# Dividing a ring of thirteen buffers among three kinds of tile, and issuing the loads of a unit earlier, in a chunked RWKV-7 scan

## The chip, the cores and the metric

The kernel runs on one core of a Trainium2 chip. The metric is the device time of one execution in microseconds (us). Three executions of the kernel before gave 4045.82, 4052.56 and 4052.54 us; their median is 4052.54. One more execution was taken with the hardware profiler; it took 4050.69 us, and every row below is from that one.

A core has five engines that follow their own instruction streams: PE (TensorE, matmuls; its weight loads are listed apart as PEld), DVE (VectorE), ACT (ScalarE), POOL (GpSimd) and SP (SyncE, which here issues nearly all DMAs). Each stream runs strictly in its own order. Streams meet at semaphores.

## The reference

A trunk of two layers works on 512 latent tokens and 256 context tokens of 1024 channels. Every layer is a half-SwiGLU, a token mixer, and another half-SwiGLU. Layer 0 mixes with HGRN2, layer 1 with a bidirectional RWKV-7. The change lies in the scan of layer 1, which computes, for 16 heads of 64 channels and both directions:

```
def step(s, inp):
    dec, kt, vt, kkt, bt = inp[:5]
    sa = jnp.einsum('bhvk,bhk->bhv', s, kkt)
    s = s * dec[:, :, None, :] - sa[..., None] * bt[:, :, None, :] + vt[..., None] * kt[:, :, None, :]
    y = jnp.einsum('bhvk,bhk->bhv', s, inp[5]) if with_out else None
    return s, y
...
for n, reverse in enumerate((False, True)):
    yc_n, s_ctx = rwkv_scan(dec_c, k_c, vc, kkc, b_c, rc, s0, reverse)
    y_n, _ = rwkv_scan(dec_l, k_l, v, kk, b_l, r, s_ctx, reverse)
```

So the latent scan of a direction begins from the state that the context scan of that direction ends with. The reference goes token by token. The kernel computes the same in chunks of 64 tokens: what a chunk does to the state is an affine map, which needs the inverse of a triangular 64x64 matrix for each head, chunk and direction.

## The kernel before

**Units.** `rwkv_scan` (from L1183) cuts the work into 12 units. A unit is four heads (a quarter of the channels) and 256 tokens in both directions: the context first, then one half of the latent tokens, then the other. Unit i is called u0 to u11 here. The state G goes from unit to unit within a quarter. A unit is four chunks of 64 tokens.

**Stages of a unit.** Each is a Python generator that yields between small steps:

- `prep_a` (L1225 on) loads KR (kk and r), `ld` (b and k, 256 KB for each of four DMAs) and hw. PE makes the decays (`sw`, L1258), ACT a tanh, DVE `sg` (L1262), PE running sums (`cum`, L1271), ACT the exponentials E and Ei, DVE scales KR by E (L1285) and makes BK from ld and Ei (L1288). PE multiplies BK by KR (`A`, L1311), and DVE masks the product into N and Ar (L1317). DVE transposes the second direction's N into NT (L1322). SP writes the 32x32 diagonal blocks of N and NT to DRAM (`md`, L1325).
- `prep_m` loads the blocks back in another layout (`M<-md`, L1337). POOL inverts them in 30 steps, each a product `mt` (L1343) and a sum `M` (L1344), and writes the inverse to DRAM (`me`, L1347).
- `prep_d` loads the inverse into P with eight DMAs (L1357).
- `prep_b` loads VU (L1366), transposes BK on PE (L1375) and forms KW (L1388).
- `prep_c` begins with DVE transposing P: first `PT0`, 128x512, for the first direction, then 128x1024 for the second (both L1397). PE joins the two halves of each inverse (TT, L1415, and Yo, L1417), ACT and DVE copy the result back (DVE: L1429), and new KR come out (L1458, L1460).
- `scan` is the chain over the chunks: PE products and DVE `G` (L1492), and outputs `y` (DVE L1512). `readout` (L1515 on) normalizes the output of a finished quarter.

**What sets the order.** The loop at the end of `rwkv_scan` takes a step of `scan(i)` and between them steps of the fillers: inversions of later units, the preparation, and the readout. The preparation of iteration i is a chain of pieces that the letters of `SEQ = 'Adabc'` set: the first two steps of `prep_a(i+2)`, `prep_d(i+1)`, the rest of `prep_a(i+2)`, `prep_b(i+1)`, `prep_c(i+1)`. From that the scheduler of the framework decides the final order of each engine's instructions with a timeline of its own and priorities (`urgent`). So a change in the loop or in the buffers can move any instruction of the scan. Within the trace the order on an engine is fixed.

**Buffers.** KR, BK and Ar take tiles of 512 KB (128x1024 floats) from one ring of 13 buffers in turn (`Q`, L1194). Until the pool B2 is opened, the ring serves N, NT and M too. A tile is written when all readers of the buffer's last tile are done. A unit uses two KR, two BK and two Ar.

Of the kernel before, what the change touches and what calls it, by code (L numbers as in the profile page):

```python
# [9 lines left out]
F32 = mybir.dt.float32  # L10
# [13 lines left out]
I32 = mybir.dt.int32  # L24
RMS_EPS = 1e-6
GN_EPS = 64e-5
NQ1, NQ2, NG = 13, 11, 6
RM, RP, RO, RV, RF = 6.0, 9.0, 0.6, 1.5, 1.3
NPRO = 12
ORDERED = {mybir.EngineType.PE, mybir.EngineType.DVE, mybir.EngineType.Activation}  # L30
LO = True
RX = 0.12
# [15 lines left out]
NBA, NBS, NB = 2, 4, 2  # L48
TCKW = dict(schedule_with_timeline_sim=True)
HP = 800, 400, 800  # L50
SEQ = 'Adabc'
Q1 = ("KR", "BK", "Ar")


V_NORM = 0
# [18 lines left out]
def trunk(ctx, tc, io, phases=None, dump=None):  # L74
# [1108 lines left out]
    def rwkv_scan(l):  # L1183
        nonlocal work, wt, hpool, psw
        B1 = open_pool("B1")
# [6 lines left out]
        late = {}  # L1192

        def Q(name):  # L1194
            if name == "N" and "B2" in late:
                return late["B2"].tile([128, 1024], F32, tag="N", name=name, bufs=4)
            first = "B2" not in late or name in Q1
            return (B1 if first else late["B2"]).tile([128, 1024], F32, tag="Q", name=name, bufs=NQ1 if first else NQ2)

        turn = cycle(range(NB))  # L1200

# [30 lines left out]
        def prep_a(qd, g):  # L1232
# [7 lines left out]
            KR, BK, N, Ar = ([None, None] for _ in range(4))  # L1240
# [3 lines left out]
            for d in range(2):  # L1244
# [7 lines left out]
                for i in range(2):  # L1252
                    nc.sync.dma_start(out=ld[:, i], in_=src(S[f"bk{d}"][i]))
                lds.append(ld)

                p = bank("sw", "a")
                for m in range(2):
# [313 lines left out]
        for _ in both(second, chain(prep_d(*todo[0]), prep_b(*todo[0]), prep_c(*todo[0]))):  # L1571
            pass
        inversions = chain(*(prep_m(*k) for k in todo[1:]))
        for i, k in enumerate(todo):
            ahead = stage(prep_a, i + 2)
            ahead = urgent(ahead, HP[1])
            parts = {"A": islice(ahead, 2), "a": ahead, "b": stage(prep_b, i + 1), "c": urgent(stage(prep_c, i + 1), HP[2]), "d": urgent(stage(prep_d, i + 1), HP[2])}
            prep = chain(*(parts[x] for x in SEQ))
            due = [0.0] * 3
            for _ in urgent(scan(*k, *ready.pop(k)), HP[0]):  # L1580
                for n, (f, r) in enumerate(((inversions, RM), (prep, RP), (out, RO))):
                    due[n] += r
                    while due[n] >= 1.0:
                        due[n] -= 1.0
                        next(f, None)
            for _ in prep:
                next(inversions, None)
            if k[1] == 2:
                for _ in out:
                    pass  # L1590
                out = readout(k[0], state["y"], to_dram)
# [189 lines left out]
```

## Time and profile before

| | us |
|---|---|
| median of three executions | 4052.54 |
| profiled execution | 4050.69 |
| its span | 4048.9 |
| PE busy | 3533.1 (87%) |
| DVE busy | 2501.8 (62%) |
| POOL busy | 1354.0 (33%) |
| ACT busy | 1314.0 (32%) |

The span is what the engines' rows cover; 1.8 us of the execution lie around it. The shares are means over very different stages. The scan of layer 1, with the preparation, takes the stretch from about 2845 to 3530 us, and there the picture is another one than on average, as the windows below show. In the rows below the first number is the start in us from the beginning of the span, the second the duration in us, and what stands in brackets is the idle time of the engine ahead of this instruction and what ended it. "x2" is a count of instructions that the row joins. A line of SPq is a transfer: the DMA queue that SP feeds.

### The profile page before, as it was taken

What the parts mean: (1) busy time and instruction counts of PE and PEld (TensorE: products, weight loads), DVE (VectorE), ACT (ScalarE), POOL (GpSimd) and SP (SyncE); (2) the same over time, 40 slices, a digit from 0 to 9 for tenths busy, and PEclk for the clock granted to TensorE, in tenths of its full rate; (3) what the DMA queues carried; (4) which work ended last, traced back from release to release, by engine and by line L of the source; (5) the groups of instructions that cost most, each with busy time, mean ns of one, the idle gap of its engine ahead of it and who ended that gap; (6) DMA issues with size and microseconds to landing.
All of it is one profiled execution on the core that took longest, in us unless ns stands there. A gap on an engine that the chain in (4) does not pass through costs nothing.

```text
span 4048.9 us, 65631 instructions
## 1 busy us (share of the span) xinstructions
PE 3533.1 (87%) x26882; PEld 3120.3 (77%) x26882; DVE 2501.8 (62%) x4072; ACT 1314.0 (32%) x2032; POOL 1354.0 (33%) x1383
## 2 busy tenths in 40 slices
PE   5999997899997999998999996989666667598998
PEld 3999986788885988887999985768555656577887
DVE  6666677566567666567766666763332434268886
ACT  4333333232233333234333333543211212134343
POOL 3222224343344222223222215223635353514332
PEclk9999998999998999998999997989878777798999
DMA  5332321411111333332322222476221312132332
GB/s 185 116 95 85 110 75 40 115 42 42 42 42 60 99 112 107 104 101 71 95 89 87 90 80 68 151 244 157 64 71 44 86 41 72 40 110 72 96 95 83
DMA packets 517066, 362.77 MB, mean 90 GB/s; under 512 B 83517, under 2 KB 490333, under 8 KB 516766
## 3 DMA queue, kind: packets, MB, share of 16 engines
q1 hardware_dynamic: 514654, 353.34, 29.5%
q8 instruction: 211, 3.46, 0.4%
q0 software_dynamic: 960, 3.15, 0.4%
q10 hardware_dynamic: 1152, 2.10, 0.1%
q14 instruction: 89, 0.73, 0.1%
HBM read 315.64 MB, written 42.87 MB: 89 GB/s over the span
## 4 chain that ended last, share of the span: by engine, by line
PE 29%; POOL 9%; issue 8%; DVE 5%; DMA 1%; ACT 1%; SPq 0%; DVEq 0%; POOLq 0%; ACTq 0%
PE po L607 8%; PE c L534 5%; POOL M L1344 4%; POOL mt L1343 4%; PE a L534 4%; PE b L534 3%; PE v L222 1%; PE k L222 1%; PE o L222 1%; DVE wlo L527 1%; DVE mx L960 1%; PE A L1311 1%; PE a L1085 0%; DMA tv<-s_xv 0%; DVE wlo L197 0%
## 5 line engine op out<-in xcount | busy, mean ns | idle before, releaser
L607 PE MATMUL po<-g,whi 128*128 128x512 f32 (+1 forms) x2464 | 592.6, 350 | 10.6 <-ACT g L211 10.2
L551 POOL TENSOR_TENSOR raw<-raw 128x512 f32<-128x512 f32 x88 | 126.0, 1431 | 1348.5 <-DMA raw<-in_ffn_w_in 686.1
L534 PE MATMUL c<-u,whi 128*128 128x386 f32 (+1 forms) x2112 | 522.9, 331 | 50.9 <-DVE uu L565 15.6
L526 ACT ACTIVATE whi<-raw 128x1024 fp32r<-128x1024 f32 x352 | 332.5, 950 | 573.8 <-PE po L607 307.7
L607 PEld LDWEIGHTS po<-g,whi 128*128 128x128 f32 x2464 | 405.8, 190 | 84.9 <-issue 11.4
L527 DVE TENSOR_TENSOR wlo<-raw,whi 128x1024 fp32r<-128x1024 f32 x352 | 419.2, 1195 | 32.2 <-ACT whi L526 30.1
L534 PEld LDWEIGHTS c<-u,whi 128*128 128x128 f32 x2112 | 370.4, 190 | 77.9 <-ACT u L446 30.2
L534 PE MATMUL a<-u,whi 128*128 128x386 f32 (+1 forms) x1408 | 349.5, 332 | 22.6 <-DVE u L428 17.2
L607 PE MATMUL po<-g,wlo 128*128 128x512 f32 (+1 forms) x1232 | 366.8, 348 | 0.0
L611 DVE SCALAR_TENSOR_TENSOR h<-po,mod,h 128x512 f32<-128x512 f32 (+1 forms) x384 | 228.2, 628 | 193.9 <-PE po L607 193.9
L534 PE MATMUL b<-u,whi 128*128 128x386 f32 (+1 forms) x1408 | 343.4, 328 | 2.5 <-DVE u L449 1.4
L534 PE MATMUL c<-u,wlo 128*128 128x386 f32 (+1 forms) x1056 | 344.3, 326 | 0.0
L1343 POOL TENSOR_TENSOR mt<-M 64x30 f32<-64x30 f32 (+4 forms) x360 | 180.6, 502 | 402.4 <-DMA M<-md 288.4
L534 PEld LDWEIGHTS a<-u,whi 128*128 128x128 f32 x1408 | 253.5, 194 | 28.3 <-issue 18.4
L196 ACT ACTIVATE whi<-raw 128x1024 fp32r<-128x1024 f32 (+1 forms) x193 | 184.5, 959 | 265.8 <-PE c L534 110.0
L534 PEld LDWEIGHTS b<-u,whi 128*128 128x128 f32 x1408 | 246.0, 189 | 12.0 <-issue 6.6
L534 PE MATMUL a<-u,wlo 128*128 128x386 f32 (+1 forms) x704 | 233.9, 332 | 0.5 <-DVE wlo L527 0.5
L534 PE MATMUL b<-u,wlo 128*128 128x386 f32 (+1 forms) x704 | 229.2, 326 | 1.9 <-DVE wlo L527 1.9
L607 PEld LDWEIGHTS po<-g,wlo 128*128 128x128 f32 x1232 | 207.7, 190 | 29.8
L197 POOL TENSOR_TENSOR wlo<-raw,whi 128x1024 fp32r<-128x1024 f32 x48 | 127.1, 2650 | 301.1 <-ACT whi L196 273.1
L1490 PE MATMUL G<-G,KR 64*64 64x64 f32 x640 | 43.7, 260 | 205.3 <-DVE G L1492 121.3
L534 PEld LDWEIGHTS c<-u,wlo 128*128 128x128 f32 x1056 | 203.0, 192 | 0.0
(366 smaller groups left out, 7434.5 us busy)
## 6 DMA issues: line engine op xcount, KB each, us to landing
raw<-in_ffn_w_in SPq DMA_DIRECT2D x176, 512.0 KB
raw<-in_mod_w SPq DMA_DIRECT2D x144, 512.0 KB
raw<-in_ffn_w_out SPq DMA_DIRECT2D x80, 384.0 KB
raw<-in_hgrn_w_in SPq DMA_DIRECT2D x40, 512.0 KB
raw<-in_ffn_w_out SPq DMA_DIRECT2D x28, 512.0 KB
raw<-in_w_rkv SPq DMA_DIRECT2D x24, 512.0 KB
ld<-s_bk SPq DMA_DIRECT2D x48, 256.0 KB
s_bk<-knb SPq DMA_DIRECT2D x32, 192.0 KB
```

The lines of the kernel that those rows point to most:

```text
L196: act.activation(hi[:, :m], raw[:, :m], AF.Copy)
L197: slots["lo"].tensor_tensor(lo[:, :m], raw[:, :m], hi[:, :m].bitcast(F32), ALU.subtract)
L222: pe.matmul(p[:, q:q + t1 - t0], a[:, k, c0:c0 + 128], b[:, t0:t1], start=(k == 0 and i == 0), stop=(k == nk - 1 and i == 2))
L526: act.activation(hi, x, AF.Copy)
L527: dve.tensor_tensor(lo, x, hi.bitcast(F32), ALU.subtract)
L534: pe.matmul(p[:, :q], a[:, c], x[k][:, b], start=first and k == 0 and i == 0, stop=k == 3 and i == 2, skip_group_check=not first)
L551: pool.tensor_tensor(S[:, lo], U[:, lo], U[:, hi], ALU.add)
L607: pe.matmul(p[v][:, :t1 - t0], wx[:, k, at:at + 128], x[:, e, t0:t1], start=k == 0 and i == 0, stop=k == nk - 1 and i == 2)
L611: dve.scalar_tensor_tensor(h[d][:, t0:t1], p[v][:, :t1 - t0], mods[l, sub, 2][:, d, v:v + 1], h[d][:, t0:t1], ALU.mult, ALU.add)
L1343: eng.tensor_tensor(t, M[:, 0:j, j:j + 1].to_broadcast([64, j, n]), M[:, j:j + 1, j + 1:32].to_broadcast([64, j, n]), ALU.mult)
L1344: eng.tensor_tensor(M[:, 0:j, j + 1:32], M[:, 0:j, j + 1:32], t, ALU.add)
L1490: pe.matmul(p[half(hp), at(d, e)], KR[d][half(hp), 4 * e + cs[d], 0], G[half(hp), 2 * d + e], start=False, stop=True, skip_group_check=True)
```

## The change

The one ring is divided: KR gets six buffers, BK three and Ar four, again 13 in all (before B2 opens, N shares the ring of Ar, and NT and M that of KR). In `prep_a` the loads of both directions are issued first, in a step of their own, and the loop calls that step for unit i+3 at the head of iteration i; the other steps of `prep_a` remain at i+2. `SEQ` goes, and the order of the pieces is now: loads of unit i+3, four steps of `prep_a(i+2)`, `prep_b(i+1)`, `prep_d(i+1)`, the rest of `prep_a(i+2)`, `prep_c(i+1)`. The number of steps of unit 1 that are taken in the prologue is 10, not 12.

```
-NQ1, NQ2, NG = 13, 11, 6
+RINGS, NQ2, NG = {"KR": 6, "BK": 3, "Ar": 4}, 11, 6
-NPRO = 12
+NPRO = 10
-SEQ = 'Adabc'
-Q1 = ("KR", "BK", "Ar")
...
         def Q(name):
-            if name == "N" and "B2" in late:
-                return late["B2"].tile([128, 1024], F32, tag="N", name=name, bufs=4)
-            first = "B2" not in late or name in Q1
-            return (B1 if first else late["B2"]).tile([128, 1024], F32, tag="Q", name=name, bufs=NQ1 if first else NQ2)
+            if name not in RINGS:
+                if "B2" in late:
+                    if name == "N":
+                        return late["B2"].tile([128, 1024], F32, tag="N", name=name, bufs=4)
+                    return late["B2"].tile([128, 1024], F32, tag="Q", name=name, bufs=NQ2)
+                ring = "Ar" if name == "N" else "KR"
+            else:
+                ring = name
+            return B1.tile([128, 1024], F32, tag=ring, name=name, bufs=RINGS[ring])
...
                 lds.append(ld)
+            yield
+            for d in range(2):
...
+        third = stage(prep_a, 2)
+        next(third)
         for i, k in enumerate(todo):
-            ahead = stage(prep_a, i + 2)
-            ahead = urgent(ahead, HP[1])
-            parts = {"A": islice(ahead, 2), "a": ahead, "b": stage(prep_b, i + 1), "c": urgent(stage(prep_c, i + 1), HP[2]), "d": urgent(stage(prep_d, i + 1), HP[2])}
-            prep = chain(*(parts[x] for x in SEQ))
+            ahead, third = urgent(third, HP[1]), stage(prep_a, i + 3)
+            b, c, d = stage(prep_b, i + 1), urgent(stage(prep_c, i + 1), HP[2]), urgent(stage(prep_d, i + 1), HP[2])
+            prep = chain(islice(third, 1), islice(ahead, 4), b, d, ahead, c)
```

Up to the scan no engine's order differs, and POOL's order is the same throughout. In the scan the instructions are the same and their order differs on PE, DVE, ACT and SP. Three places follow. The line numbers of the kernel after are up to five higher there (NT is L1327, PT L1402, BK L1293, the load of M L1342).

**DVE, where the NT of u6 is made.** In the kernel before, PT0 of u5 and the small instructions of a reciprocal root stand ahead of these rows (G is the state of the scan of u4, N the masked product of u6, sg and what stands behind it the preparation of u7, BK in the second row that of u6):

```order
L1492 TENSOR_TENSOR G<-G,gt 128x256 x2
L1288 TENSOR_TENSOR BK<-ld,Ei 128x8x64 x2
L1492 TENSOR_TENSOR G<-G,gt 128x256
L1317 TENSOR_TENSOR N<-A,cst_21938 128x256 x4
L1322 STREAM_TRANSPOSE NT<-N 128x1024
L1262 TENSOR_SCALAR sg<-sg 128x512 x2
L1285 TENSOR_TENSOR KR<-KR,E 128x512 x2
L1299 COPY gt<-E 128x2
L1288 TENSOR_TENSOR BK<-ld,Ei 128x8x64
L1295 TENSOR_TENSOR gt<-E,Ei 128x2x3
L1288 TENSOR_TENSOR BK<-ld,Ei 128x8x64
```

In the kernel after the same place, from the PT0 on:

```order
L1402 STREAM_TRANSPOSE PT_26094<-P_10_21948 128x512
L1497 TENSOR_TENSOR G<-G,gt 128x256
L1322 TENSOR_TENSOR N<-A,cst_21938 128x256 x4
L1267 TENSOR_SCALAR sg<-sg 128x512 x2
L1290 TENSOR_TENSOR KR<-KR,E 128x512 x2
L1304 COPY gt<-E 128x2
L1293 TENSOR_TENSOR BK<-ld,Ei 128x8x64
L1300 TENSOR_TENSOR gt<-E,Ei 128x2x3
L1293 TENSOR_TENSOR BK<-ld,Ei 128x8x64
L1305 COPY gs<-Ei 128x2
L1327 STREAM_TRANSPOSE NT<-N 128x1024
```

The chain sg, KR, BK of the next unit's first direction, which stood behind NT, now stands ahead of it, and three of the four G rows and the BK of u6 stand ahead of PT0 rather than behind it.

**SP, the same unit.** md<-NT and md<-N write the blocks of u6, M loads them, hw_s and ld belong to u7 in the kernel before and to u8 in the kernel after, VU to an earlier unit, P_00 is the load of the inverse of u6. Before:

```order
L1325 DMA md<-NT 32x8x32 x4
L1239 DMA hw_s<-s_hw 65x256 x2
L1253 DMA ld<-s_bk_20093 128x2x256 x2
L1253 DMA ld<-s_bk_20094 128x2x256 x2
L1337 DMA M<-md 64x1024
L1325 DMA md<-N 32x8x32 x4
L1357 DMA P_00_21946<-me 32x8x32 x4
```

After:

```order
L1371 DMA VU<-s_v 64x4x128 x2
L1242 DMA hw_s<-s_hw 65x256 x2
L1256 DMA ld<-s_bk_20093 128x2x256 x2
L1330 DMA md<-NT 32x8x32 x4
L1342 DMA M<-md 64x1024
L1330 DMA md<-N 32x8x32 x4
L1362 DMA P_00_21946<-me 32x8x32 x4
```

M stood behind hw_s and four loads of ld; it stands right behind md<-NT now. One pair of ld, of 512 KB, stands ahead of md<-NT.

**DVE, the tail: the last inverse, of u11.** G is the scan of u10, PT the transposes of the inverse of u11, and the COPY rows take what PE made of them. Before:

```order
L1492 TENSOR_TENSOR G<-G,gt 128x256
L1397 STREAM_TRANSPOSE PT_29803<-P_10_21948 128x512
L1492 TENSOR_TENSOR G<-G,gt 128x256 x3
L1397 STREAM_TRANSPOSE PT<-P_11_21949 128x1024
L1429 COPY P_10_21948<-Yo 32x8x32
L1429 COPY PT<-Yo 32x8x32
```

After:

```order
L1497 TENSOR_TENSOR G<-G,gt 128x256 x3
L1402 STREAM_TRANSPOSE PT_29803<-P_10_21948 128x512
L1497 TENSOR_TENSOR G<-G,gt 128x256
L1402 STREAM_TRANSPOSE PT<-P_11_21949 128x1024
L1434 COPY P_10_21948<-Yo 32x8x32
L1434 COPY PT<-Yo 32x8x32
```

Two of the G rows have moved from behind the first PT to ahead of it.

## Rows read from the trace of the kernel before

**Rows 1.** The head of the profile's page, and, from the chain that ended last, the shares of the span by line.

```profile
span 4048.9 us, 65631 instructions
...
PE po L607 8%; PE c L534 5%; POOL M L1344 4%; POOL mt L1343 4%; PE a L534 4%; PE b L534 3%; PE v L222 1%; PE k L222 1%; PE o L222 1%; DVE wlo L527 1%; DVE mx L960 1%; PE A L1311 1%; PE a L1085 0%; DMA tv<-s_xv 0%; DVE wlo L197 0%
```

**Rows 2.** Windows: the stretch in us, its length, the busy time (and count) of PE, PEld, DVE, ACT and POOL, the granted clock of PE as a share of 2.4 GHz, the busy share of the DMA engines, GB/s.

```profile
2845.00:3530.00 685.00, 442.40 (x7759) 389.10 (x7758) 233.56 (x594) 132.34 (x325) 339.11 (x682) 0.78 0.23 57
3151.00:3165.00 14.00, 13.09 (x206) 11.75 (x206) 9.78 (x25) 7.06 (x17) 0.00 (x0) 1.00 0.59 160
3207.00:3221.00 14.00, 7.38 (x74) 6.31 (x74) 5.37 (x12) 0.81 (x1) 0.00 (x0) 0.50 0.53 140
```

**Rows 3.** Waits in the stretch 2885 to 3535 us: who waits, for what; us in total, times, the longest.

```profile
POOL mt L1343 <- DMA M<-md: 288.4, 10, 37.8
DVE PT L1397 <- DMA P<-me: 245.5, 11, 25.8
```

**Rows 4.** Timeline of POOL: the first step of the inversion of u6, the store of its result, and the first step of the inversion of u7.

```profile
3169.60 0.24 POOL L1343 TENSOR_TENSOR mt<-M 64x30 f32<-64x30 f32 x1 [34.05 <-DMA M<-md]
...
3204.06 0.58 POOL L1347 DMA_DIRECT2D me<-M  x1 [0.30 <-POOL M L1344]
...
3231.06 0.64 POOL L1343 TENSOR_TENSOR mt<-M 64x30 f32<-64x30 f32 x1 [26.42 <-DMA M<-md]
```

**Rows 5.** Timeline of DVE. The NT of u2, u3, u5, u6, u7, u8, u9 and u11 in this order; ahead of those of u2, u6, u7 and u11 the PT0 of the unit before; and behind the NT of u6 and of u7 the last BK of the next unit's first direction.

```profile
2890.91 0.71 DVE L1397 STREAM_TRANSPOSE PT<-P 128x512 f32<-128x512 f32 x1 [22.00 <-DMA P<-me]
...
2892.85 1.22 DVE L1322 STREAM_TRANSPOSE NT<-N 128x1024 f32<-128x1024 f32 x1
...
2957.44 1.25 DVE L1322 STREAM_TRANSPOSE NT<-N 128x1024 f32<-128x1024 f32 x1
...
3087.72 1.23 DVE L1322 STREAM_TRANSPOSE NT<-N 128x1024 f32<-128x1024 f32 x1
...
3140.77 0.71 DVE L1397 STREAM_TRANSPOSE PT<-P 128x512 f32<-128x512 f32 x1 [21.99 <-DMA P<-me]
...
3153.67 1.25 DVE L1322 STREAM_TRANSPOSE NT<-N 128x1024 f32<-128x1024 f32 x1
...
3160.44 0.68 DVE L1288 TENSOR_TENSOR BK<-ld,Ei 128x512 f32<-128x512 f32 x1
...
3209.65 0.71 DVE L1397 STREAM_TRANSPOSE PT<-P 128x512 f32<-128x512 f32 x1 [24.41 <-DMA P<-me]
...
3222.52 1.23 DVE L1322 STREAM_TRANSPOSE NT<-N 128x1024 f32<-128x1024 f32 x1
...
3230.91 0.68 DVE L1288 TENSOR_TENSOR BK<-ld,Ei 128x512 f32<-128x512 f32 x1
...
3285.86 1.23 DVE L1322 STREAM_TRANSPOSE NT<-N 128x1024 f32<-128x1024 f32 x1
...
3353.28 1.25 DVE L1322 STREAM_TRANSPOSE NT<-N 128x1024 f32<-128x1024 f32 x1
...
3471.96 0.71 DVE L1397 STREAM_TRANSPOSE PT<-P 128x512 f32<-128x512 f32 x1 [22.78 <-DMA P<-me]
...
3484.51 1.23 DVE L1322 STREAM_TRANSPOSE NT<-N 128x1024 f32<-128x1024 f32 x1
```

**Rows 6.** Timeline of the DMA queue of SP: the load of M for u2, u3, u5, u6, u7, u8, u9 and u11 in this order, and one pair of ld.

```profile
2897.28 0.48 SPq L1337 DMA_DIRECT2D M<-md  x1
...
2971.24 0.67 SPq L1337 DMA_DIRECT2D M<-md  x1
...
3095.87 0.48 SPq L1337 DMA_DIRECT2D M<-md  x1
...
3164.75 1.56 SPq L1337 DMA_DIRECT2D M<-md  x1
...
3227.56 0.48 SPq L1337 DMA_DIRECT2D M<-md  x1
...
3296.34 0.89 SPq L1253 DMA_DIRECT2D ld<-s_bk  x2
3297.27 0.48 SPq L1337 DMA_DIRECT2D M<-md  x1
...
3364.42 0.47 SPq L1337 DMA_DIRECT2D M<-md  x1
...
3489.44 0.48 SPq L1337 DMA_DIRECT2D M<-md  x1
```

**Rows 7.** Timeline of PE: products A and decays sw, the first two rows beside the NT of u6, the other two beside that of u7.

```profile
3151.57 1.60 PE L1311 MATMUL A<-KR,BK 64*128 64x64 f32 x16
3153.19 1.99 PE L1258 MATMUL sw<-w_s,hw_s 65*128 65x256 f32 x8
...
3217.14 2.24 PE L1311 MATMUL A<-KR,BK 64*128 64x128 f32 x12
...
3222.95 3.62 PE L1258 MATMUL sw<-w_s,hw_s 65*128 65x256 f32 x8
```

**Rows 8.** The tail, timelines of DVE and of PE: the PT0 of u11, the first copy of the joined inverse, and, on PE, the first of the products TT.

```profile
3534.66 0.71 DVE L1397 STREAM_TRANSPOSE PT<-P 128x512 f32<-128x512 f32 x1 [21.67 <-DMA P<-me]
...
3547.62 0.41 DVE L1429 COPY P<-Yo 32x256 f32<-32x256 f32 x1 [6.39 <-PE Yo L1417]
```

```profile
3545.24 0.22 PE L1415 MATMUL TT<-PT,N 32*32 32x32 f32 x2
```

## Prediction, made before the changed kernel was run

> **What bounds the kernel now.** I read the page first: the span and the chain that ended last [rows 1]. Over the whole span PE dominates that chain, but the two lines of POOL's inversion, L1344 and L1343, hold 8% of it together, and they run in the scan alone. The windows then show that in the 685 us of the scan PE works 442 us at a mean granted clock of 0.78, while POOL is busy half the time [rows 2]. The waits say what POOL does in the other half: it waits 288.4 us, ten times, for the load of M, and DVE waits 245.5 us, eleven times, for P, which is the inverse [rows 3]. So two waits face each other, and the timelines give their circle. The inversion of u6 runs from 3169.60 to the store at 3204.06, 34.5 us, during which the rest soon runs dry; PT0 of u6 starts at 3209.65; only then the work goes on that leads to the NT of u7 (3222.52); M is loaded at 3227.56, and the next inversion begins at 3231.06 [rows 4 to 6]. The scan's length is eleven inversions of that size and ten gaps between them. The change touches no instruction of POOL, so what it does to the time is what it does to the gaps. I cut each gap in four: store to PT0 (5.59 us here), PT0 to NT, NT to the load of M, load to first step (3.50 here).
>
> The announced part, loads three units ahead, I cost at nothing: with six KR buffers and two per unit, the KR of unit i+3 still waits for the scan of unit i to release its buffers, as a KR loaded into the ring of 13 had to; and `ld` has two buffers in both kernels. What moves is the order, and three places of it count.
>
> **A: NT to the load of M.** The load waits in SP's stream behind what stands ahead of it. In u2, u7 and u11, and likewise in u4 and u10, that is next to nothing: 4.43 us in u2, 5.04 in u7, 4.93 in u11 [rows 5, 6]; the five together 23.91, a mean of 4.78. In u3, u5, u6, u8 and u9 it stands behind loads of ld, whose buffers come free only when the next unit's BK is made, later on DVE than NT: 13.80, 8.15, 11.08, 11.41 and 11.14 us, 55.58 together [rows 5, 6]. In the new order M is right behind md in every unit but u5, where one pair of ld lies between. That takes 55.58 - 5 x 4.78 = 31.7 us: **-31.7**.
>
> **B: ld ahead of md.** In u2, u3, u4, u6, u7 and u9 a pair of ld of 512 KB now stands right ahead of md<-NT, and in u5 between md and M. These loads have their buffers by then, since BK stands ahead of NT now. The nearest row is a pair of ld that took 0.89 us on the queue, with M less than 1 us behind its start [rows 6]: 7 x 0.9 = **+6.3**. The lower bound is 0, where the loads run beside the transpose. For the upper one: the load of M in u6, right behind four ld, took 4.85 us to the first step of POOL, that in u7 without them 3.50 [rows 4, 6]; half of the difference more for each pair, 7 x (0.9 + 0.7) = 11.
>
> The Trainium skill speaks against this part of the change: on its page "DMA: Bandwidth & Descriptors", section "Queues, rings and completion order", it says that each DMA engine consumes the descriptors of a queue in ring order, so that 512 KB put ahead of the small md would have to go first. At the 160 GB/s of a busy stretch [rows 2] 512 KB take 3.3 us, seven times 23, and the sum would be about +4 rather than the one below. The 1.35 us by which four ld delayed M in u6 agree in sign but are far from two times 3.3, so I keep 6.3.
>
> **C: PT0 to NT.** Before, the ten stretches take 115.7 us together: 1.94 in u2, 12.90 in u6, 12.87 in u7, 12.55 in u11 [rows 5], the others between 9 and 15. In the new order the NT of u2, u3, u4, u5, u6, u7, u9 and u10 stands on DVE behind the chain of the next unit's first direction: sw on PE, tanh on ACT, sg on DVE, cum on PE, the exponentials, KR, BK. Those of u8 and u11 have a part of it ahead. Before, that chain ran behind NT, and from the first sw to the end of the last BK it took 3161.12 - 3153.19 = 7.9 us in u6 and 3231.59 - 3222.95 = 8.6 in u7 [rows 5, 7]. NT needs nothing of it; it waits by its place. Against that, much that stood between PT0 and NT (G of the scan, the unit's BK, half of N and Ar) now stands ahead of PT0, where DVE idles some 22 us anyway [rows 5], so it is free there.
>
> So I go through each unit, taking what is left between PT0 and sw and adding the chain. In u6 PT0, one G, four N and the A that they wait for are left: 0.71, and for the rest the 1.60 us of 16 A at the full clock [rows 5, 7] and about as much again for the masks, 3.5 to 4 in all; plus 8, so 12. In u7 the outputs y and 16 A remain, at the half clock (12 A took 2.24 us there [rows 7]); I take nearly the old stretch, 12.5, and 8.6: 21, and u10, built the same way, 21. In u2 1.4 and 8.6: 10. In u3 8.8 and 8.2: 17, in u4 6.5 and 8: 14.5, in u9 6.8 and 8.2: 15. In u5 all A stand ahead of PT0, sw has run, and the rear of the chain takes 5. In u8 12 and in u11 9, from two half-sets of A, their masks, and the part of the chain that stands there. The heads of these sums (1.4, 8.8, 6.5, 6.8) are estimates: the instructions left, counted by kind, by the rows of like instructions at the clock that a stretch behind a stall has. Sum 136.5, against 115.7: **+20.8**. Bounds: with every instruction behind PT0 at the full clock the same counts give 117.4, that is +1.7; with the half clock through the whole first 10 us, 150.3, that is +34.6.
>
> **D: the tail.** After the last inversion only PT0 of u11 and what hangs on it remain. Before, 12.96 us pass from PT0 to the first copy of the joined inverse, since G, two transposes and products of the old scan stand ahead of TT, which begins at 3545.24 [rows 8]. After, two G stand ahead of PT0, and PE has TT soon behind the second transpose: 0.71, half a us for the G between, 1.25 as for NT of that size [rows 5], and the 2.38 from TT to the copy [rows 8], 4.8 together: **-8**. I give it 0 to -9.
>
> The first two inversions and everything outside the scan are cost at nothing, within 2 us, since the order there is the same.
>
> **Sum.** -31.7 + 6.3 + 20.8 - 8 = -12.6 us. Against the profiled execution of 4050.69 that is 4038.1; the median of the runs lies 1.85 above that execution, so 4040. Its own range goes from 4029 to 4050, by half of the way to C's bounds on either side. A measurement of this kernel can tell about 0.2%, 8 us, from no change.
>
> **Rivals.** *Paid back (no change):* the half clock holds after each stall. It stood at 0.50 in the 14 us before the NT of u7, and at 1.00 behind that of u6, where PE was busy 13 of 14 us [rows 2]. If it holds, C is +34.6, and the sum +1.2: 4054; with B at nothing 4048. Against it: less work is left between PT0 and NT in most units. Chance 0.24.
>
> *The chain uncovered (slower):* one mechanism: NT behind the next unit's sw, tanh, sg, cum, exponentials and BK, with nothing moved ahead in exchange, as the moved work needs KR and VU that come late, or runs behind PT0 all the same. Then eight units pay 8.2 us each, 66, and the sum is -31.7 + 6.3 + 66 - 8 = +33: 4085. It decides from the point at which C is over 33, which is half of the 66 uncovered. For it: the chain is serial over three engines, and DVE's order is strict. Against it: DVE has 22 us of idle time ahead of each PT0. Chance 0.2.
>
> *PE kept warm (faster):* the scan's products run on while POOL inverts, so PE idles less before PT0 and keeps its full clock behind it. Then C is +1.7, B near 0, and the sum -38: 4015. For it: at the full clock the same products took 1.60 for 16 A against 2.24 for 12 [rows 7]. Against it: the moved work is short beside 22 us, so PE stalls all the same. Chance 0.2. The Trainium skill's page "TensorE: Matmul & The Clock Gate", section "Part 1: The HAM clock gate", has the clock throttled by default and released by activity; the two windows agree with it (0.50 and 1.00), and by it this rival stands or falls with what PE does just ahead of PT0.
>
> **Chances.** The forecast has 0.36. Faster by over 0.2%, that is under 4044, holds two thirds of the forecast and the warm rival with a part that lies between: 0.54. Within 0.2%: 0.24. Slower: 0.22. The range reaches from 4010, below the warm rival, to 4066, past the one of no change and into the slower one, and leaves out the slow end.
>
> **What would show it.** A is right if NT to M is near 5 us in every unit of the new trace, POOL's wait for M falls below the 288 us by 10 or more, and wrong if M waits for another thing in SP's stream. C shows in PT0 to NT: 10 to 21 us, longest in u7 and u10. B shows as md<-NT that starts over 1 us later behind NT than before. D shows as the last PT0 to the first copy in under 6 us. A sum over 150 us for C, or KR loads that now end the wait of the chain, would make the prediction wrong.

## The result and the profile after

The kernel after takes 4077.41 us (median of three executions, 4070.35 to 4078.45) against 4052.54 before: a ratio of 1.0062, with a 95% interval of 1.0039 to 1.0085. It is 25 us slower, where 12 us less had been forecast. Its profiled execution took 4078.45 us, 27.8 more than that of before (4050.69).

Where the time went can be read in the order of the prediction. The head of the page and the chain that ended last, after:

```profile
span 4076.7 us, 65636 instructions
...
PE po L605 8%; PE c L532 5%; POOL M L1349 5%; POOL mt L1348 4%; PE a L532 4%; PE b L532 3%; PE k L220 1%; PE o L220 1%; DVE mx L958 1%; DVE wlo L525 1%; PE a L1083 0%; PE A L1316 0%; DVE wlo L195 0%; DMA tv<-s_xv 0%; PE modp L250 0%
```

POOL's inversion has 9% of the chain now, where it had 8 [rows 1]. Windows with the columns of [rows 2], the scan first (here it ends about 3560), then what follows it:

```profile
2845.00:3560.00 715.00, 526.61 (x8078) 452.88 (x8064) 239.95 (x599) 141.07 (x338) 335.76 (x673) 0.75 0.21 55
3560.00:4076.00 516.00, 449.40 (x3206) 404.22 (x3206) 394.93 (x638) 199.05 (x295) 157.38 (x116) 0.92 0.30 92
```

POOL works about as long as before (335.76 us for 339.11), the stretch is 30 us longer, and PE's mean clock is lower, 0.75 for 0.78. PE's rows in it, 8078 for 7759, show 527 us of busy time for 442. All that follows the last inversion is about 6 us shorter. POOL's waits after, against the 288.4 us of [rows 3]:

```profile
POOL mt L1348 <- DMA M<-md: 258.2, 8, 45.1
POOL mt L1348 <- PE Yo L1422: 33.5, 1, 33.5
POOL mt L1348 <- PE A L1316: 27.6, 1, 27.6
```

Two of the ten waits are put down to PE rather than to the load of M, so the three lines go together: 319.3 us, that is 30.9 more than before. The ten gaps between inversions, cut as the prediction cut them, show which part grew. Each number is the sum over u2 to u11, taken from the starts of the rows in the timelines of POOL, DVE and SP; the stretch from PT0 to NT is cut once more, at the end of the last N or Ar of the unit (the last mask). Where that mask stands ahead of PT0, as in u5 of the kernel after, the cut is at the end of PT0.

| us, ten gaps | store to PT0 | PT0 to last mask | last mask to NT | NT to load of M | load to first step | sum |
|---|---|---|---|---|---|---|
| before | 57.2 | 116.1 | -0.5 | 79.5 | 41.9 | 294.2 |
| after | 56.2 | 92.2 | 87.8 | 52.6 | 36.3 | 325.1 |

(A row's end overlaps the start of the next a little, hence -0.5.) Before, NT followed the last mask at once. After, it follows 88 us later, summed over the units (in u11 it still follows at once). DVE beside the NT of u7, after, where [rows 5] has 12.87 us from PT0 to NT:

```profile
3220.80 0.71 DVE L1402 STREAM_TRANSPOSE PT<-P 128x512 f32<-128x512 f32 x1 [17.41 <-DMA P<-me]
...
3238.49 0.41 DVE L1322 TENSOR_TENSOR Ar<-A,cst 128x256 f32<-128x256 f32 x1
3242.04 0.43 DVE L1267 TENSOR_SCALAR sg<-sg 128x512 f32<-128x512 f32 x1 [3.14 <-ACT sg L1266]
3244.88 0.43 DVE L1267 TENSOR_SCALAR sg<-sg 128x512 f32<-128x512 f32 x1 [2.41 <-ACT sg L1266]
3248.45 1.29 DVE L1290 TENSOR_TENSOR KR<-KR,E 128x512 f32<-128x512 f32 x2 [3.14 <-ACT E L1278]
...
3250.41 0.68 DVE L1293 TENSOR_TENSOR BK<-ld,Ei 128x512 f32<-128x512 f32 x1
...
3251.08 1.24 DVE L1327 STREAM_TRANSPOSE NT<-N 128x1024 f32<-128x1024 f32 x1
```

All that NT needs is there at 3238.90. DVE then waits three times, for tanh, tanh and the exponentials of u8, and NT starts at 3251.08, 30.28 us behind PT0. No row shows NT waiting for anything: it has no bracket. A stall by place is seen only in the brackets of the instructions ahead of it. On PE, in the same stretch:

```profile
3236.04 2.07 PE L1316 MATMUL A<-KR,BK 64*128 64x128 f32 x8
3238.04 1.33 PE L1391 MATMUL W<-VU,N 64*64 64x64 f32 x20
3239.30 2.07 PE L1263 MATMUL sw<-w_s,hw_s 65*128 65x256 f32 x4
...
3245.01 1.22 PE L1389 MATMUL kT<-cst,KR 64*64 64x64 f32 x17
```

and its windows, in which the clock's column is the third from the right:

```profile
3220.00:3232.00 12.00, 8.93 (x80) 7.71 (x80) 5.62 (x13) 0.00 (x0) 0.00 (x0) 0.50 0.53 147
3232.00:3244.00 12.00, 12.00 (x90) 9.74 (x89) 1.94 (x5) 2.28 (x4) 0.00 (x0) 0.50 0.15 45
3244.00:3252.00 8.00, 7.99 (x139) 6.82 (x139) 3.98 (x9) 4.14 (x11) 0.00 (x0) 0.72 0.06 20
```

PE is at 1.2 GHz through the first 24 us of it (the mean of the third window is 0.72), with the products kT and W of another piece between the steps of the chain: four sw take 2.07 us, where eight took 1.99 at the full clock [rows 7]. What the prediction hoped of SP came true. M stands right behind md (and ld no longer between):

```profile
3251.12 0.38 SPq L1256 DMA_DIRECT2D ld<-s_bk  x1
...
3252.07 0.43 SPq L1256 DMA_DIRECT2D ld<-s_bk  x1
3252.59 2.24 SPq L1330 DMA_DIRECT2D md<-NT  x4
3257.11 0.47 SPq L1342 DMA_DIRECT2D M<-md  x1
```

And the tail, where [rows 8] has 12.96 us from PT0 of u11 to the first copy, takes 5.00:

```profile
3568.96 0.71 DVE L1402 STREAM_TRANSPOSE PT<-P 128x512 f32<-128x512 f32 x1 [20.96 <-DMA P<-me]
...
3573.96 0.41 DVE L1434 COPY P<-Yo 32x256 f32<-32x256 f32 x1 [1.32 <-PE Yo L1422]
```

The account closes. The inversion of u1 ends 3.1 us later than before, the ten gaps are 30.9 longer, the ten inversions 0.1; the last one ends 34.1 later, and what follows it is 6.3 shorter: 27.8, the difference of the two profiled executions.

### The profile page after: what moved, and what is told of

It is laid out like the page before. It is cut to its first block, busy times and chain, and to the rows that moved or that the text cites. A ratio compares the mean times of both kernels' runs of the same rounds, so it can differ in the third digit from the quotient of the medians.

```text
span 4076.7 us, 65636 instructions
## 1 busy us (share of the span) xinstructions
PE 3606.9 (88%) x26882; PEld 3175.4 (78%) x26882; DVE 2516.3 (62%) x4072; ACT 1316.8 (32%) x2032; POOL 1356.0 (33%) x1383
## 4 chain that ended last, share of the span: by engine, by line
PE 27%; POOL 10%; issue 10%; DVE 5%; DMA 1%; ACT 1%; SPq 0%; POOLq 0%; DVEq 0%; ACTq 0%
PE po L605 8%; PE c L532 5%; POOL M L1349 5%; POOL mt L1348 4%; PE a L532 4%; PE b L532 3%; PE k L220 1%; PE o L220 1%; DVE mx L958 1%; DVE wlo L525 1%; PE a L1083 0%; PE A L1316 0%; DVE wlo L195 0%; DMA tv<-s_xv 0%; PE modp L250 0%
## 5 line engine op out<-in xcount | busy, mean ns | idle before, releaser
L532 PE MATMUL c<-u,whi 128*128 128x386 f32 (+1 forms) x2112 | 523.0, 331 | 49.4 <-ACT u L444 14.6
L525 DVE TENSOR_TENSOR wlo<-raw,whi 128x1024 fp32r<-128x1024 f32 x352 | 415.5, 1184 | 32.9 <-ACT whi L524 30.9
L195 DVE TENSOR_TENSOR wlo<-raw,whi 128x768 fp32r<-128x768 f32 (+1 forms) x145 | 177.7, 1226 | 46.1 <-ACT whi L194 46.0
```

Of the source, the lines that this page charges most:

```text
L195: slots["lo"].tensor_tensor(lo[:, :m], raw[:, :m], hi[:, :m].bitcast(F32), ALU.subtract)
L525: dve.tensor_tensor(lo, x, hi.bitcast(F32), ALU.subtract)
L532: pe.matmul(p[:, :q], a[:, c], x[k][:, b], start=first and k == 0 and i == 0, stop=k == 3 and i == 2, skip_group_check=not first)
```

## The experiments

Theory 1, formed from these rows: the loss is NT's place on DVE, behind the next unit's sg, KR and BK. Theory 2: it is PE at the half clock with its work behind PT0, wherever NT stands. Theory 3: it is the divided rings or the early loads themselves. The kernel before was timed again beside each group of experiments; its medians were 4052.13 (beside e1 to e4), 4054.27 (e5 to e8) and 4051.53 us (e9 to e12).

| run | median us | ratio to before, 95% interval |
|---|---|---|
| e1 after, NT in its own buffer | 4055.22 | 1.0007 (0.9998 to 1.0017) |
| e2 rings alone | 4056.17 | 1.0010 (1.0001 to 1.0020) |
| e3 loop alone | 4065.25 | 1.0035 (1.0020 to 1.0050) |
| e4 M loaded by POOL | 4027.49 | 0.9943 (0.9928 to 0.9958) |
| e5 NT late, in the kernel before | 4061.76 | 1.0020 (1.0010 to 1.0029) |
| e6 order of the pieces (control of e5) | 4040.75 | 0.9966 (0.9955 to 0.9978) |
| e7 NT ahead of PT0 | 3973.09 | 0.9801 (0.9784 to 0.9817) |
| e8 e7, md by ACT, M by POOL | 3970.15 | 0.9794 (0.9779 to 0.9808) |
| e9 after, NT ahead of PT0 | 4004.99 | 0.9884 (0.9870 to 0.9899) |
| e10 e7, P by ACT | 4002.85 | 0.9879 (0.9865 to 0.9894) |
| e11 after, NT own and ahead, P by ACT | 4008.42 | 0.9894 (0.9878 to 0.9911) |
| e12 e10 with e6's order | 3982.80 | 0.9825 (0.9809 to 0.9841) |

The gaps of the runs that carry the verdicts, in the columns of the table above. For e5 and e6 they are those of u2 to u10 alone, as e5 leaves u11 out. Where NT stands ahead of PT0 the cut at NT makes no sense, and only the first column and the sum are given. The columns come from the one execution that was profiled; in e2 and e6 it took 4061.36 and 4046.75 us, 5 and 6 us more than the median.

| us | store to PT0 | PT0 to last mask | last mask to NT | NT to load of M | load to first step | sum |
|---|---|---|---|---|---|---|
| e1 | 56.9 | 126.7 | -0.4 | 64.8 | 37.2 | 285.1 |
| e2 | 56.8 | 131.9 | -0.4 | 75.9 | 39.8 | 304.0 |
| e3 | 56.9 | 94.3 | 49.6 | 61.1 | 37.2 | 299.1 |
| e4 | 57.3 | 117.3 | -0.5 | 55.6 | 36.3 | 266.0 |
| e5, nine gaps | 51.2 | 40.1 | 119.4 | 43.5 | 32.8 | 287.0 |
| e6, nine gaps | 51.2 | 99.9 | -0.4 | 71.0 | 37.5 | 259.2 |
| e7 | 58.1 | | | | | 218.7 |
| e9 | 158.7 | | | | | 234.9 |
| e10 | 115.7 | | | | | 241.4 |

### e1: NT out of the shared ring

In the kernel after NT takes its tile from the ring of eleven that BKT, KW, PT and M share once B2 is open. With a buffer of its own, paid for by cutting that ring to ten, the scheduler puts NT right behind the masks again; the rest of the change stays.

```diff
                 if "B2" in late:
-                    if name == "N":
-                        return late["B2"].tile([128, 1024], F32, tag="N", name=name, bufs=4)
+                    if name in ("N", "NT"):
+                        return late["B2"].tile([128, 1024], F32, tag=name, name=name, bufs=4 if name == "N" else 1)
...
-RINGS, NQ2, NG = {"KR": 6, "BK": 3, "Ar": 4}, 11, 6
+RINGS, NQ2, NG = {"KR": 6, "BK": 3, "Ar": 4}, 10, 6
```

> The kernel after, with NT in a buffer of its own (one) and the ring of the pool B2 cut from 11 to 10. With it NT stands on DVE right behind the last N or Ar again, ahead of the next unit's sg, KR and BK; the loads, the rings and the loop stay as in the kernel after. Theory 1 (place: the loss is the chain that NT was put behind): the ten stretches from PT0 to NT fall from 180 us to 95 to 120, M stays within 6 us of NT, and the time falls by 60 to 80 us to 4000 to 4017. Theory 2 (the loss is PE at the half clock and its work behind PT0, wherever NT stands): the stretches stay over 160 us and the time within 10 us of 4077.

It took 4055.22 us, 22 less than the kernel after, and not told apart from before. The stretch from the last mask to NT went from 87.8 us to nothing, as theory 1 has it. But the other columns moved against it: PT0 to the last mask grew by 35 us, NT to M by 12, and what follows the last inversion is 7 us longer again (520.9 for 513.5): from the last PT0 to the first copy it is 11.80 us, with a second G behind PT0 and, on PE, products of other pieces (bkt, kT, W) ahead of TT. So PT0 to NT fell from 180 to 126, not to the 95 to 120 expected, and the time by 22 us rather than 60 to 80. In u7 the NT stands right behind the last mask, and yet 23.96 us behind PT0:

```profile
3219.36 0.41 DVE L1322 TENSOR_TENSOR Ar<-A,cst 128x256 f32<-128x256 f32 x1
3219.69 1.24 DVE L1327 STREAM_TRANSPOSE NT<-N 128x1024 f32<-128x1024 f32 x1
```

```profile
3197.00:3209.00 12.00, 12.00 (x110) 9.77 (x108) 2.54 (x6) 0.00 (x0) 0.00 (x0) 0.50 0.25 69
3209.00:3221.00 12.00, 12.00 (x92) 10.32 (x92) 4.88 (x11) 0.60 (x1) 0.00 (x0) 0.50 0.37 112
```

There PE is busy for 24 us without a break at the half clock, with G, y, 32 A, BK's transposes and kT ahead of the last A. So theory 2 has a share too: when NT is free of the chain, PE's row of products is what ends last in u7, at 1.2 GHz throughout, and in u10, where the mean clock from PT0 to NT is 0.60.

### e2 and e3: the two halves of the change

e2 takes the rings alone (the new `Q` in the kernel before), e3 the loads and the loop alone (the old `Q` in the kernel after).

> The kernel before with the thirteen buffers divided (6, 3, 4) and nothing else of the change: loads and order of the pieces as before. In its order NT stands behind no sg, but behind all G and the unit's BK; M has at most one pair of ld ahead. Theory 1 (place): A and B as forecast, no chain ahead of NT, so 20 to 30 us faster than before, 4022 to 4032. Theory 3 (the division itself makes tiles wait for each other): 4052 or slower, with waits of KR or BK loads ahead of NT.

> The kernel after with one ring of thirteen buffers again: only the early loads and the new order of the pieces. In its order sg of the next unit stands ahead of NT in seven units, but not KR and BK; M stands right behind md in most units. Theory 1 (place): half of the chain (sw, tanh, sg) costs 3 to 5 us in seven units, some 28 us, against A of -27 and less work behind PT0: 4035 to 4060. Theory 3 (the rings): the loss of the kernel after is gone, under 4030. If the loop alone is at 4077, the loop and not the rings carries the loss.

e2 is at 4056, barely slower than before. Theory 1 foretold 20 to 30 us faster, and that missed: I had taken "at most one pair of ld ahead of M" for free. It is not. NT to the load of M is 75.9 us for 79.5, because that one pair waits just as well for the BK of the next unit. The queue of SP beside the M of u8 in e2:

```profile
3288.88 2.89 SPq L1330 DMA_DIRECT2D md<-NT  x4
...
3297.78 0.90 SPq L1258 DMA_DIRECT2D ld<-s_bk  x2
3298.85 0.48 SPq L1342 DMA_DIRECT2D M<-md  x1
```

The pair starts 6.0 us behind the end of the md rows, and M right behind it. The rest of the miss stands in another column: PT0 to the last mask is 131.9 us for 116.1. DVE's waits in e2, from 2885 to 3545 us, show a wait of the kind that theory 3 names, BK waiting until PE's transposes (bkt) have read an older BK:

```profile
DVE BK L1293 <- PE bkt L295: 18.4, 9, 3.8
```

Before, that was one wait of 3.4 us. Five of the nine, 14.6 us together, fall between PT0 and NT; before, BK waits 5.5 us there for PE. So with three buffers for BK the division does make tiles wait, and theory 3 is borne out in e2. In the kernel after BK waits 6.8 us for bkt, in five waits, and none of them falls between PT0 and NT: there this wait is not the loss.

e3, at 4065, is 13 us slower than before, 5 us above the 4035 to 4060 of theory 1 and far from the under 4030 of theory 3. In seven units sg, and no BK, stands ahead of NT, and the stretch from the mask to NT is 49.6 us. Neither half gives the 25 us: the two losses, 4 and 13 us, add to 17.

### e4: term A by itself

```diff
-            nc.sync.dma_start(out=M, in_=md)
+            pool.dma_start(out=M, in_=md)
```

> The kernel before with one edit: the load of M is issued by POOL, not by SP, so it no longer stands behind ld. The order on DVE is nearly that of the kernel before. Term A alone: NT to the first step of POOL falls from 79.5 + 41.9 us in ten units to some 85, that is 27 to 37 us less, if the load issued by POOL costs no more than 1 us over that by SP: 4016 to 4026. Rival: what M waited for on SP was hidden or the load by POOL starts later by 3 us a unit: within 8 us of 4052.

4027.49 us: 25 less than before, 1.5 above the range of 4016 to 4026. NT to the load falls from 79.5 to 55.6, load to first step by 5.6 more, and the ten inversions grow by 4.5. They grow by 3.9 and 5.0 in e1 and e3 too, where SP issues the load; why is open. The queue of SP still has four ld behind the md of u6, and they start late as before. But M no longer stands behind them: POOL issues it at 3153.75, ahead of the ld.

```profile
3149.97 1.81 SPq L1325 DMA_DIRECT2D md<-NT  x4
3151.87 0.78 SPq L1239 DMA_DIRECT2D hw_s<-s_hw  x2
3156.17 3.56 SPq L1253 DMA_DIRECT2D ld<-s_bk  x4
```

```profile
3153.75 0.52 POOL L1337 DMA_DIRECT2D M<-md  x1 [22.69 <-ACT Ei L1274]
```

So A was a real cost of the kernel before, and the change did take it off. What the change adds must be larger.

### e5 and e6: the place alone, in the kernel before

The end of `prep_a` that makes NT and md is kept back for u2 to u10, until the next unit's first BK is there. To hold it there, one element of BK is copied into NT's tile, which the transpose then overwrites. No ring is divided, and no load comes earlier. e6 is the control, as e5 needs another order of the pieces.

```diff
-SEQ = 'Adabc'
+SEQ = 'Aadbc'
...
+            def finish(after=None):
+                if after is not None:
+                    dve.tensor_copy(NT_[0:1, 0, 0:1], after[0:1, 0, 0, 0:1])
...
+                if d == 0 and waiting:
+                    with tc.high_priority(offset=400):
+                        waiting.pop()(BK[0])
```

> The kernel before (one ring, loads not earlier) with NT and md of u2 to u10 put, by an added dependency, behind the next unit's first BK, and, as that needs it, the pieces in the order A, a, d, b, c. So the place of NT of the kernel after without its rings and without its early loads; M then stands right behind md as well. Theory 1 (place): NT starts 8 to 13 us behind the last mask in most units, 80 to 95 us in all as in the kernel after (88); part of it is paid back, since M no longer waits behind ld (-25) and fewer masks stand behind PT0 (-20 to -40): 20 to 45 us slower than the control e6, that is 4065 to 4095. Theory 3 (the rings or the early loads carry the loss): within 8 us of the control.

> The control for e5: the kernel before with the pieces in the order A, a, d, b, c and nothing else. NT stands right behind the last mask as before; on SP the load of M is freed of ld in two more units (u6 and u10). Theory 1: 5 to 20 us faster than before, 4032 to 4047, by those two units. If the order of the pieces alone cost what the kernel after costs, it would be 4070 or more.

e5 is 21.0 us slower than its control, at the near end of 20 to 45 (4061.76 itself lies 3 us below the 4065 to 4095 that went with it). In the nine units that it moves, the stretch from the last mask to NT is 119.4 us, more than the 80 to 95 expected and the 88 of the kernel after, for here NT often stands behind the chain of the second direction and the second transpose too. Of that 59.8 us are paid back between PT0 and the last mask and 27.5 between NT and M; u11, which has nothing ahead of its NT, gains 9 more. DVE beside the NT of u6 in e5:

```profile
3160.46 0.42 DVE L1321 TENSOR_TENSOR N<-A,cst 128x256 f32<-128x256 f32 x1 [0.49 <-PE A L1315]
3164.20 0.43 DVE L1263 TENSOR_SCALAR sg<-sg 128x512 f32<-128x512 f32 x1 [3.31 <-ACT sg L1262]
3167.03 0.43 DVE L1263 TENSOR_SCALAR sg<-sg 128x512 f32<-128x512 f32 x1 [2.41 <-ACT sg L1262]
...
3177.00 1.23 DVE L1329 STREAM_TRANSPOSE NT<-N 128x1024 f32<-128x1024 f32 x1
```

The picture is that of the kernel after. e6 is 13.5 us faster than before, within its range, but not through the two units that I had named: over the ten gaps NT to M is only 3.6 us less, and PT0 to the last mask 6.6. The place alone thus costs about what the change as a whole loses, 21 us against 25, without the rings and without the early loads. So neither is needed for a loss of this size, though NT stands further back here than in the kernel after.

### e7 to e9: the same place, used the other way

If NT's place between PT0 and M is what makes the gaps, putting NT ahead of PT0 should take the 116 us of the kernel before out of them. e7 adds one small copy, by which PT0 depends on the next unit's NT; the transpose that follows overwrites it.

```diff
+            ahead = turned_n.get((qd + (g + 1) // 3, (g + 1) % 3))
+            if ahead is not None:
+                dve.tensor_copy(PT[0][0:1, 0, 0:1], ahead[0:1, 0, 0:1])
             for d in range(2):
                 dve.transpose(PT[d], P1[d][:, :, :32 + 32 * d])
```

> The kernel before with a one-element copy that makes PT0 of a unit depend on the NT of the next one, so that all that stands between the two on DVE (masks, G, BK) must run ahead of PT0, while POOL still inverts. Theory 1 (the gap is what DVE's order puts between PT0 and NT): these 116 us go from the gaps; md still waits on SP behind the load of P, which waits for the inverse, so 5 to 8 us a gap remain that were hidden, and M waits for ld in five units: 40 to 100 us faster, 3950 to 4010. Rival (the work behind PT0 stands there because its data come late): PT0 itself is held back by as much, and the time is within 10 us of 4052 or slower.

> As e7, and the stores md are issued by ACT, the load of M by POOL, so that neither stands behind the load of P or of ld on SP. Theory 1: the gap of a unit falls to the store of the inverse, the load of M and their latency, 6 to 10 us instead of 29, so some 150 to 200 us faster: 3850 to 3900. Rival (PE becomes the bound of the scan: 442 us of work of which a part runs at the half clock; or ACT's stores hold up ACT): the gain stays under 100 us, 3950 or more.

> The kernel after with the one-element copy of e7 (PT0 depends on the next unit's NT). NT keeps its place behind the next unit's sg, KR and BK, but both now stand ahead of PT0, under the inversion. Theory 1 (place): the 180 us between PT0 and NT leave the gaps; md waits on SP behind the load of P and costs some 22 us a gap as in e7: 3960 to 4000, within 25 us of e7. Rival (the chain of the next unit, now ahead of PT0 as well, is longer than the inversion and holds PT0 back): 4020 or more.

e7 takes 3973 us, 2% less than before, and the gaps fall by 75.5 us, not by the whole 116. DVE beside the NT of u7: it is made while POOL inverts, and PT0 of u6 starts 2.8 us behind the start of its load.

```profile
3156.82 1.24 DVE L1322 STREAM_TRANSPOSE NT<-N 128x1024 f32<-128x1024 f32 x1
...
3158.49 0.14 DVE L1399 COPY PT<-NT 1x1 f32<-1x1 f32 x1
3169.46 0.71 DVE L1401 STREAM_TRANSPOSE PT<-P 128x512 f32<-128x512 f32 x1 [10.83 <-DMA P<-me]
```

What is left of the gap, 22.6 us of idle POOL here, is now SP's. md of u7, ready at 3158.06, stands behind the load of P, which waits for the inverse, and behind what else has queued up:

```profile
3166.68 3.75 SPq L1358 DMA_DIRECT2D P<-me  x8
...
3173.06 2.60 SPq L1367 DMA_DIRECT2D VU<-s_v  x3
...
3178.36 2.64 SPq L1326 DMA_DIRECT2D md<-NT  x4
...
3183.29 0.48 SPq L1338 DMA_DIRECT2D M<-md  x1
```

e8, which takes md and M off SP, wins no more: 3970, at 3850 to 3900 expected. Its gaps are 205 us for 219, and the inversions 7 us longer. ACT's stream is not free either: from the end of NT to the first md row 10.1 us pass on the mean of the ten units, for 17.7 on SP in e7. Two of POOL's waits:

```profile
POOL M L1338 <- DMA md<-NT: 56.7, 3, 19.9
POOL M L1338 <- ACT E L1273: 49.9, 3, 18.3
```

The rival written down for it, that the gain stays under 100 us, holds; which of its two reasons it is (PE, or ACT held up) these rows do not settle between them. e9 puts the same copy into the kernel after. It gains 72 us on it, but stays 32 us behind e7, outside the 25 that theory 1 allowed, and at 4005 between its 3960 to 4000 and the 4020 of the rival. Here the chain of the next unit holds back PT0 itself: store to PT0 is 158.7 us for 58.1. What the chain waits for is its KR (DVE's waits, 2885 to 3485 us):

```profile
DVE KR L1290 <- DMA KR<-s_kk: 104.2, 7, 21.9
```

Ahead of the PT0 of u6, for one, SP issues the first KR load at 3193.94, behind the load of P at 3185.32, which waits for the inverse.

### e10 to e12: what is left

The loads of P go to ACT's queue:

```diff
-                nc.sync.dma_start(out=P1[d][r0:r0 + 32, 8 * hp:8 * hp + 8, 32 * b:32 * b + 32], in_=me[l0:l0 + 8].rearrange("l s t -> s l t"))
+                nc.scalar.dma_start(out=P1[d][r0:r0 + 32, 8 * hp:8 * hp + 8, 32 * b:32 * b + 32], in_=me[l0:l0 + 8].rearrange("l s t -> s l t"))
```

> e7 (the kernel before and the copy) with the eight loads of P issued by ACT, so that md and M no longer stand on SP behind loads that wait for the inverse. If SP's order is what is left of the gap (22 us in e7): M is loaded while POOL inverts, the gaps of most units fall under 8 us, and the time to 3840 to 3900. Rival (ACT, held at the load of P until the inverse is there, holds up what PE and DVE need): 3950 or more, no better than e7.

> The kernel after with NT in a buffer of its own, the copy of e7 and the loads of P on ACT: the change put to use where NT and SP no longer hold it. If the early loads and the divided rings are worth something once NT is out of the way: 5 to 30 us faster than e10. If they are worth nothing (the KR of a unit wait for the same scan): within 10 us of e10.

> e10 with the pieces in the order A, a, d, b, c, as in e6. If the order of the pieces is worth here what it was worth alone (13 us): 10 to 15 us faster than e10; if what it saved was the wait of M behind ld, which e10 hides under the inversion: within 6 us of e10.

e10 is 30 us slower than e7: the rival. The wait only went to another engine, which has more to do behind it, and this is what ACT waits for:

```profile
ACT ybuf L1546 <- DMA P<-me: 66.6, 2, 34.0
ACT sg L1261 <- DMA P<-me: 63.4, 2, 34.3
```

e11, with the whole change in and NT and SP freed of it, is 5.6 us above e10 (4008.42 against 4002.85): the early loads and divided rings are worth nothing there. e12 is 20 us faster than e10, where 10 to 15 or under 6 was expected: the order of the pieces is worth more there than alone, and why is open.

## Why the prediction was wrong

**What bounds the scan** was read rightly. POOL's work did not change, and the 30.9 us that POOL waits longer are the loss. That the announced part, the earlier loads, gives nothing agrees with e5, which has a loss of that size without it, and with e11, which has no gain with it.

**A and B** held. Forecast: -31.7 and +6.3, so -25.4. Measured: -26.9 between NT and M and -5.6 between M and POOL's first step, -32.5. B, the ld ahead of md, cost little: M stands 5.3 us behind NT on the mean, where the freed units of before had 4.78, and from the load to POOL's first step it is 0.6 us less. The larger price that the prediction gave beside its own, 3.3 us for each pair of ld, did not appear. The row behind B was misread, though: a line of SPq is SP's issuing of a DMA, not its transfer. From 3296.30 to 3297.20, the time of the pair of ld in [rows 6], the DMA engines moved 10 GB/s, and from there to 3300.00 they moved 260; and the issue of a 32 KB md has a row as long as that of a 256 KB ld, 0.4 us. So 0.9 us is what a pair costs in SP's stream; what its bytes cost those that follow was not priced. e4 confirms A by itself, with 25 us.

**D** held: -8 forecast, 12.96 to 5.00 us from the last PT0 to the first copy, and 6.3 less in all behind the last inversion.

**C failed.** The step is the one that goes through each unit, "taking what is left between PT0 and sw and adding the chain": +20.8 was forecast, the ten stretches came to 180.0 us instead of 136.5, that is +64.3. The mechanism was right and stood in the text with its eight units. Both sizes in it were too small:

- *The chain.* In the eight units where it was priced, at 5 to 8.6 us, 63 together, the stretch from the last mask to NT measures 84.4. The 7.9 us came from a stretch at the full clock, the 8.6 from one at the half clock in which PE had almost nothing else to do [rows 5, 7]. In the new order the chain mostly meets both, the half clock and the kT and W of another piece between its steps: from the first sw at 3239.30 to the end of BK at 3251.09 it is 11.8 us beside the NT of u7, at a mean clock of 0.61.
- *The heads.* What is left between PT0 and the last mask in those units measures 73.1, where 52.4 were estimated: 18.1 in u7 for 12.5, 11.6 in u4 for 6.5. The instructions were counted, but the products of other pieces between them were not: in u7 and in u4 eight bkt and 26 kT stand on PE ahead of and among the last 16 A, for some 4 us.

Both are one mistake: each stretch was priced by its own instructions, without the products that stand between them on PE, and at the half clock these count. Four windows, each from the first sw of a chain to the end of its second BK, tell the two apart; the first two are of the kernel before, beside the NT of u7 and of u2, the others of the kernel after, beside that of u3 and of u4:

```profile
3222.95:3231.59 8.64, 8.45 (x30) 7.13 (x30) 4.30 (x10) 4.66 (x12) 0.53 (x1) 0.51 0.33 80
2892.41:2903.66 11.25, 11.21 (x104) 9.99 (x104) 5.10 (x12) 5.77 (x15) 2.35 (x5) 0.65 0.41 98
2967.10:2974.85 7.75, 7.72 (x110) 6.00 (x104) 3.50 (x10) 4.76 (x12) 0.00 (x0) 1.00 0.08 23
3037.51:3049.31 11.80, 11.80 (x105) 9.44 (x104) 3.51 (x10) 4.70 (x11) 0.00 (x0) 0.50 0.08 24
```

With some 80 other products the chain takes 7.75 us at the full clock and 11.80 at the half; with almost none, 8.64 at the half. The second window had both in the trace of before, 11.25 us, and would have been the row to price the chain by. The bound on C of 14 us for the half clock (136.5 to 150.3) was too small for the same reason.

Two slips of the working change nothing: by its own rule, half of the way to C's bounds, the inner range ends at 4047 at most and not at 4050; and the two rows of A that the warm rival compares have 64 and 128 columns (16 A of 128 columns take 1.68 us at 3161.34 of the same trace, for 1.60, so the comparison stands).

**The rivals.** The outcome is the one called "the chain uncovered", forecast at 4085 with C at +66; it had 0.2. Its reason was off in one point: it said that nothing would be gained ahead of PT0 in exchange. PT0 to the last mask did fall by 24 us, and the chain cost 88. "PE kept warm" had it the wrong way round, as the mean clock fell from 0.78 to 0.75. The range ended at 4066, short of this rival's 4085, though the working had counted its eight units.

**What the prediction did not see** is that A and C are one thing. In the kernel before M waited behind ld, and ld waited for the BK of the next unit; [rows 5, 6] have it, the last BK of that chain at 3160.44 and the M of u6 at 3164.75. The change did not take this wait away. It moved it from M, in five units, to NT, in eight, and there NT has md and M still ahead of it. A saving that comes from no longer waiting for a chain, and a price for waiting for the same chain elsewhere, have to be counted as one sum.

What stays open: why the scheduler puts NT behind the whole chain only with both halves of the change. e1 shows that it does so while NT takes its tile from the shared ring of B2, and not with a tile of its own. Which buffer the scheduler's own timeline waits for there is not shown.

## What to carry to other kernels

On an engine with a strict order an instruction can be late without a row that says so: look at what stands ahead of it, and price that at the clock and beside the neighbours that it will have there. When a wait goes from one queue, ask which work it waited for, and whether the same work now stands ahead of something else. And where a serial engine idles between its turns, find the instruction that starts its next turn and put it ahead of the one that waits for its last: here one copied element, which makes PT0 wait for the next NT, is worth 2%, and of all the kernels here that one and e8, which is level with it, are the fastest.

## What was not expected of the hardware

PE stayed at a granted clock of 0.50 through the 12 us from 3232 to 3244 of the kernel after, in which its rows show it busy for 12.00 us without a gap, and in e1 through 24 us, 3197 to 3221, likewise without a gap. Before, it stood at 1.00 through a stretch in which it was busy for 13.09 of 14 us [rows 2]. The ends of PE's rows are modelled by the profiler, so such a row does not prove that the array worked all the time; why the clock stayed low the runs do not tell.
